# Seven-product units of 512 columns with the products added up in PSUM, and their sums of weight blocks made by accumulating DMA transfers

## The chip, the cores and the metric

The kernel runs on one core of one Trainium2 chip. The metric is the device time of one execution in microseconds (us). Three runs of the kernel before gave 1854.23, 1854.59 and 1855.96 us; the median is 1854.59 us. The engines are TensorE (PE), VectorE (DVE), ScalarE (ACT), GpSimd (POOL) and SyncE (SP, which here only issues transfers).

## The reference

A trunk of two layers over 512 tokens of width 1024. Every layer normalizes the rows and multiplies them by one wide input matrix. Its columns feed five branches A to E, and five gate paths of 512 columns and five merge paths of 1024 columns. Each branch output is multiplied by its gate, projected, weighted by its merge gate, and added up:

```
for l in range(DEPTH):                                     # 2 layers
    xn = rms_norm(h, norm_g[l])
    (..., gates, merge) = jnp.split(xn @ w_in[l], offsets, axis=-1)
    branches = (dsa_branch(...), mla_branch(...), diff_branch(...), sgu_branch(...), memory_branch(...))
    mixed = functools.reduce(jnp.add, [
        jax.nn.sigmoid(merge[:, :, n]) * ((o * jax.nn.silu(gates[:, :, n])) @ w_branch[l, n])
        for n, o in enumerate(branches)])
    h = h + mixed @ w_out[l]
return rms_norm(h, final_norm_g)
```

All is fp32. The change concerns the products `xn @ w_in[l]` for the gate and merge columns of branches A and C alone: 512 + 1024 columns for each of the two branches, in each of two layers.

## The kernel before

**Products.** Weights are loaded as raw fp32 tiles of 512 KB by SP, and each is split in two parts: `wh` is a rounded copy made on ACT, `wl` the rest, a subtraction on DVE or POOL. Activations are split likewise (`xh`, `xl`). Every product is three matmuls (`three`, L484 to L487): high by high, high by low, low by high. What is made from one raw tile is called a granule; a plain unit takes two or more of them.

**Order of the work.** The string `ORDER` lists the units of a layer; they are traced in that order, and each engine runs its instructions in one row. The attention work is a side stream that `Pace` mixes in between products by planned times. `begin` (L428) prepares a granule: it issues the loads of the next ones on SP and starts the split of the granule after it.

**The seven stage.** At a layer's end stand the units of branches A and C (tokens after `xs`). They use seven products of half blocks instead of eight. The rows are 512 tokens by 1024; their four half blocks (token halves by row halves) are combined beforehand into `t1`, `t2`, `t3` and `t4` (`x_prep`, `x_swap`). The weights' four blocks a11, a12, a21, a22 are combined into s1 = a21 + a22, s2 = s1 - a11, a11 - a21 and a12 - s2. `unit_s` (L509 to L530) does 256 columns by 512 tokens: `seven_steps` (L363 to L390) makes the four sums on POOL (L380) and splits the seven blocks: copies on ACT (L371), subtractions on DVE or, for the second block, on POOL (L373). Each of the seven products has its own PSUM tile, of 12 matmuls of 128x256. ACT copies the first out (L526), and DVE adds the others into `st` (L528). Gates then go through a tanh (L1373) and a product on DVE (L1374), and a product with the branch output on POOL (L1375). Merge gates go through a tanh (L1414), and are multiplied with the projected branch (L1403) and added to `acc` on POOL (L1411). Each merge unit of 256 columns is followed by one granule of the branch projection (`pm<-yh,wh`), of 24 matmuls of 128x512.

Of the kernel before, what the change touches and what calls it, by code (L numbers as in the profile page):

```python
# [39 lines left out]
GSET = (1,)  # L40
WSB = True
STB = True
# [15 lines left out]
class Pace:  # L58
    """Interleaves side streams (attention) with the dense products as they are traced."""
# [68 lines left out]
class Granule:  # L128
    """Up to four 128-row blocks of 256 columns of a weight, split in two fp32r parts."""

    def __init__(self, parts, n, width=256, raws=1):
        self.parts, self.n, self.width, self.raws = parts, n, width, raws


def trunk(tc, d, out, taps=None):
# [43 lines left out]
    def f32(ap):  # L179
        return ap.bitcast(F32)  # L180
# [13 lines left out]
    # ---- input rows, small vectors, constants  # L194
# [59 lines left out]
    # ---- rotary tables  # L254
# [42 lines left out]
    def rope(eng, x, j, ct, st, outs=None):  # L297
        """x [128, 2, h, 2H], token tiles 2j and 2j+1; rotated in place or into outs."""
# [19 lines left out]
    # ---- differential lambdas  # L318
# [20 lines left out]
    # ---- long lived tiles  # L339
# [7 lines left out]
    # ---- weights  # L347
    order, state = [], {"dma": 0, "split": 0, "slot": 0}

    def issue(upto):  # L350
        while state["dma"] < min(upto, len(order)):
            g = order[state["dma"]]
            g.raw = [wp.tile([128, 4, 256], F32, tag="raw", bufs=NRAW, name="raw") for _ in range(g.raws)]
# [9 lines left out]
    def seven_steps(g):  # L363
        """Seven combinations of the four 512 x 128 blocks of a granule, split, in the order of their products."""
        r0, r1 = g.raw
        a11, a21, a12, a22 = (r[:, :, c * 128:(c + 1) * 128] for r in (r0, r1) for c in range(2))
        g.prod = []

        def put(src):
            h, lo = (z.rearrange("p (k c) -> p k c", k=4) for z in wtile())  # L370
            A.activation(h, src, AF.Copy)  # L371
            yield
            (G if len(g.prod) in GSET else V).tensor_tensor(out=lo, in0=src, in1=f32(h), op=ALU.subtract)  # L373
            g.prod.append((h, lo))
            yield

        def comb(x, y, op):
            o = (blk(F32, "ws") if WSB else pp.tile([128, 512], F32, tag="p", name="ws")).rearrange(
                "p (k c) -> p k c", k=4)
            G.tensor_tensor(out=o, in0=x, in1=y, op=op)  # L380
            return o
        yield from put(a11)
        s1 = comb(a21, a22, ALU.add)
        s2 = comb(s1, a11, ALU.subtract)
        yield from put(s2)
        yield from put(comb(a11, a21, ALU.subtract))
        yield from put(s1)
        yield from put(comb(a12, s2, ALU.subtract))
        yield from put(a22)
        yield from put(a12)  # L390

    def split_steps(g):
        if g.raws == 2:
            yield from seven_steps(g)
            return
        g.raw = g.raw[0]
        g.h, g.l = [], []
        for a in range(0, g.n, 2):
            b = min(a + 2, g.n)
            h, lo = (z.rearrange("p (k c) -> p k c", k=2) for z in wtile())  # L400
            raw, hv, lv = g.raw[:, a:b, :g.width], h[:, :b - a, :g.width], lo[:, :b - a, :g.width]
            A.activation(hv, raw, AF.Copy)  # L402
            g.h.append(h)
            yield
            (G if a else V).tensor_tensor(out=lv, in0=raw, in1=f32(hv), op=ALU.subtract)  # L405
            g.l.append(lo)
            yield
# [40 lines left out]
    def gseven(w, c0):  # L448
        def parts(*raws):
            return [(r, w[k0 * 128:(k0 + 4) * 128, c0:c0 + 256].rearrange("(k p) c -> p k c", p=128))  # L450
                    for r, k0 in zip(raws, (0, 4))]
        g = Granule(parts, 4, 256, 2)
        order.append(g)
        return g
# [29 lines left out]
    def three(o, ah, al, bh, bl, st, sp):  # L484
        T.matmul(o, ah, bh, start=st, stop=False)  # L485
        T.matmul(o, ah, bl, start=False, stop=False)  # L486
        T.matmul(o, al, bh, start=False, stop=sp)  # L487

    def unit_t(gs, kts, rh, rl, evac, n=512, ms=2):
        """[cols, tokens]: column tiles of 128."""  # L490
# [9 lines left out]
    def unit_n(gs, kts, lh, ll, evac, nt=4):  # L500
        """[tokens, cols]: token tiles in pairs, 256 columns."""
# [7 lines left out]
    def unit_s(g, xb, evac):  # L509
        """Transposed 256 columns by 512 tokens in seven products of half blocks instead of eight."""  # L510
        def run():
            begin(g)
            th = [blk(F32, "st0"), blk(F32, "st1")] if STB else [tr(name="st0"), tr(name="st1")]
            c11, c12, c21, c22 = (t_[:, a:a + 256] for t_ in th for a in (0, 256))
            uses = {"11": [(c11, None)], "t2": [(c22, c11)], "t3": [(c21, c22)], "t1": [(c12, c22), (c22, c21)],
                    "22": [(c12, c12)], "t4": [(c21, c21)], "21": [(c11, c11)]}
            for n, b in enumerate(uses):
                o = psm("s7")[:, :256]
                while len(g.prod) <= n:
                    split_some()  # L520
                for kt in range(4):
                    three(o, g.prod[n][0][:, kt], g.prod[n][1][:, kt], *xb(b, kt), kt == 0, kt == 3)
                    tick(3 * 256 * 0.43)
                for dst, other in uses[b]:
                    if other is None:
                        A.activation(dst, o, AF.Copy)  # L526
                    else:
                        V.tensor_tensor(out=dst, in0=o, in1=other, op=ALU.add)  # L528
            evac(th)
        plan.append(run)  # L530
# [13 lines left out]
    # ---- norm of rows into transposed parts  # L544
# [3 lines left out]
    def norm_rows(rows, ss, gname, l, hi, lo, step=600.0):  # L548
        """rows: [128, 1024] tiles with their sums of squares; writes hi/lo[k] [128, 128 * len(rows)]."""
# [27 lines left out]
    # ---- attention  # L577
# [27 lines left out]
    def pv_causal(o, terms):  # L605
        """terms(kb) -> list of (stationary, part of P)."""
# [8 lines left out]
    def attend(steps, scores, norm, trans, pv, pv_rows=None):  # L615
        """steps: list of (unit, i, last); software pipelined over the steps."""
# [46 lines left out]
    # ================= layers  # L663
# [20 lines left out]
    def layer(l, mm):  # L684
# [5 lines left out]
        # -- memory keys and values  # L690
# [18 lines left out]
        # -- e_q, transposed, one head per column tile  # L709
# [73 lines left out]
        # -- columns 512:1636 in natural layout  # L783
# [114 lines left out]
        # -- latent attention operands  # L898
# [116 lines left out]
        # -- sparse attention  # L1015
# [109 lines left out]
        # -- differential attention, two of its four heads at a time  # L1125
# [93 lines left out]
        # -- spatial gating  # L1219
# [106 lines left out]
        # -- combinations of the half blocks of the normed rows  # L1326
        def x_prep():
            S["t2"] = [c4(F32R, "t2").rearrange("p (k c) -> p k c", k=4) for _ in range(2)]
            for n in ("t3", "t4"):
                S[n] = [[blk(name=n).rearrange("p (k c) -> p k c", k=2) for _ in range(2)] for _ in range(2)]  # L1330
            S["t1"] = [blk(F32, "t1f").rearrange("p (k c) -> p k c", k=2) for _ in range(2)]
            for k in range(4):
                f1, f2 = tr(name="xf1"), tr(name="xf2")
                G.tensor_tensor(out=f1, in0=f32(xh[k]), in1=f32(xl[k]), op=ALU.add)
                V.tensor_tensor(out=f2, in0=f32(xh[k + 4]), in1=f32(xl[k + 4]), op=ALU.add)
                t1 = S["t1"][k // 2][:, k % 2]
                V.tensor_tensor(out=t1, in0=f1[:, 256:], in1=f1[:, :256], op=ALU.subtract)
                V.tensor_tensor(out=f1[:, 256:], in0=f2[:, 256:], in1=f1[:, 256:], op=ALU.subtract)
                V.tensor_tensor(out=f1[:, :256], in0=f2[:, 256:], in1=t1, op=ALU.subtract)
                V.tensor_tensor(out=f2[:, :256], in0=f2[:, :256], in1=f1[:, :256], op=ALU.subtract)  # L1340
                split(S["t2"][0][:, k], S["t2"][1][:, k], f1[:, :256])
                split(S["t3"][0][k // 2][:, k % 2], S["t3"][1][k // 2][:, k % 2], f1[:, 256:])
                split(S["t4"][0][k // 2][:, k % 2], S["t4"][1][k // 2][:, k % 2], f2[:, :256])
# [6 lines left out]
        def xb(b, kt):  # L1350
            if b == "t2":
                return S["t2"][0][:, kt], S["t2"][1][:, kt]
            if b in ("t3", "t4"):
# [5 lines left out]
        # -- gate, project, merge  # L1359
# [3 lines left out]
        def gates(nm, us, seven=False):  # L1363
            bi = "ABCDE".index(nm)

            def ev(ps, u):
                if u == 0:
                    y["h"] = [c4(F32R, "yh").rearrange("p (k c) -> p k c", k=2) for _ in range(2)]
                    y["l"] = [c4(F32R, "yl").rearrange("p (k c) -> p k c", k=2) for _ in range(2)]
                for m in range(2):  # L1370
                    k = 2 * u + m
                    th, sg = tr(name="th"), tr(name="sg")
                    A.activation(th, ps[m], AF.Tanh, scale=0.5)  # L1373
# [234 lines left out]
```

## Time and profile before

| what | value |
|---|---|
| median of three runs | 1854.59 us |
| the profiled execution: its own time, its span | 1854.6 us, 1854.6 us |
| PE busy | 1784.2 us, 96% of the span |
| DVE, ACT, POOL busy | 1280.2, 1000.2, 730.9 us |
| mean granted clock of PE | 0.986 |
| seven stage of layer 0 | 693.5 to 888.0 us |
| seven stage of layer 1 | 1604.1 to 1802.5 us |

The span runs from the first instruction to the last, and nothing that the profile shows lies around it. A wait is put down to the work that ended last before the waiting instruction could go. PEclk of 1.00 is the full clock of PE (2.4 GHz), 0.50 the lower one (1.2 GHz). The names in a row are those of the program: `s<-xh,wh` is a product of the seven stage, `pm` a product of any other unit, `ws` a sum of weight blocks.

### The profile page before, as it was taken

The numbers are of one execution on the slowest core, as the hardware profiler recorded it, in microseconds if no ns is written. First come the engines' busy times: TensorE is split into PE (matmuls) and PEld (weight loads), VectorE is DVE, ScalarE is ACT, GpSimd is POOL, SyncE is SP. The second block draws the span as 40 slices with busy tenths as digits, with TensorE's granted clock in tenths as the row PEclk, the third lists the DMA queues.
The fourth block names the chain that finished last, engine by engine and source line by source line (L and its number), as shares of the span: only waits on it lengthen the run. The fifth ranks groups of instructions, "written<-read, shape, count | busy, mean of one in ns | idle before, by whom it ended". The sixth has DMA issues, their size and how long they took to land. (4 is left out here: it accounts for less than half of the span.)

```text
span 1854.6 us, 31211 instructions
## 1 busy us (share of the span) xinstructions
PE 1784.2 (96%) x11481; PEld 1613.9 (87%) x11481; DVE 1280.2 (69%) x2979; ACT 1000.2 (54%) x2247; POOL 730.9 (39%) x603
## 2 busy tenths in 40 slices
PE   7999999999999997999999999999999999899898
PEld 6998889889988777989999988898999887789888
DVE  7438656996755679899354477489775655998963
ACT  7447766437745434455355567653476454444443
POOL 4123111442312366885241321125341133778733
PEclk9999999999999998999999999999999999999999
DMA  6322222332222222334452332223322222233241
GB/s 211 92 69 78 86 69 69 97 97 70 58 58 69 80 58 69 99 95 136 131 177 58 75 89 79 57 80 103 103 58 58 58 80 58 59 91 109 85 148 69
DMA packets 167745, 161.43 MB, mean 87 GB/s; under 512 B 26036, under 2 KB 163304, under 8 KB 167592
## 3 DMA queue, kind: packets, MB, share of 16 engines
q1 hardware_dynamic: 164648, 149.21, 28.0%
q0 software_dynamic: 2944, 10.23, 1.6%
q8 instruction: 91, 1.49, 0.3%
q14 instruction: 62, 0.51, 0.1%
HBM read 155.22 MB, written 4.19 MB: 86 GB/s over the span
## 5 line engine op out<-in xcount | busy, mean ns | idle before, releaser
L405 POOL TENSOR_TENSOR wl<-raw,wh 128x512 fp32r<-128x512 f32 (+1 forms) x226 | 300.8, 1332 | 803.8 <-ACT wh L402 632.8
L402 ACT ACTIVATE wh<-raw 128x512 fp32r<-128x512 f32 (+1 forms) x460 | 285.3, 623 | 328.1 <-PE pm L486 161.6
L485 PE MATMUL pm<-wh,xh 128*128 128x256 f32 x1024 | 294.6, 288 | 0.9 <-ACT nat L1091 0.8
L486 PE MATMUL pm<-wl,xh 128*128 128x256 f32 x1024 | 293.3, 286 | 0.0
L487 PE MATMUL pm<-wh,xl 128*128 128x256 f32 x1024 | 293.2, 286 | 0.0
L405 DVE TENSOR_TENSOR wl<-raw,wh 128x512 fp32r<-128x512 f32 (+1 forms) x234 | 182.7, 782 | 144.5 <-ACT wh L402 140.1
L485 PE MATMUL pm<-xh,wh 128*128 128x512 f32 x656 | 259.2, 396 | 0.8 <-ACT mth L1392 0.5
L487 PE MATMUL pm<-xh,wl 128*128 128x512 f32 x656 | 256.9, 394 | 0.0
L486 PE MATMUL pm<-xl,wh 128*128 128x512 f32 x656 | 256.7, 391 | 0.0
L485 PEld LDWEIGHTS pm<-wh,xh 128*128 128x128 f32 x1024 | 195.1, 190 | 5.8 <-ACT nat L1091 1.6
L487 PEld LDWEIGHTS pm<-wh,xl 128*128 128x128 f32 x1024 | 195.2, 191 | 2.8 <-issue 1.7
L486 PEld LDWEIGHTS pm<-wl,xh 128*128 128x128 f32 x1024 | 195.3, 191 | 2.7 <-issue 1.2
L586 ACT ACTIVATE p<-p,nm 128x512 f32<-128x512 f32 (+1 forms) x192 | 107.2, 558 | 78.2 <-DVE nm L584 77.3
L485 PEld LDWEIGHTS pm<-xh,wh 128*128 128x128 f32 x656 | 123.7, 189 | 26.8 <-ACT mth L1392 1.1
L487 PEld LDWEIGHTS pm<-xh,wl 128*128 128x128 f32 x656 | 123.6, 188 | 26.5
L486 PEld LDWEIGHTS pm<-xl,wh 128*128 128x128 f32 x656 | 123.7, 189 | 23.8
L485 PE MATMUL s<-xh,wh 128*128 128x256 f32 x384 | 113.1, 295 | 25.2 <-ACT mth L1392 12.2
L485 PE MATMUL pm<-yh,wh 128*128 128x512 f32 x320 | 125.9, 394 | 5.3 <-DVE st L528 5.3
L486 PE MATMUL pm<-yl,wh 128*128 128x512 f32 x320 | 126.0, 394 | 0.0
L487 PE MATMUL pm<-yh,wl 128*128 128x512 f32 x320 | 122.6, 392 | 0.0
L486 PE MATMUL s<-xl,wh 128*128 128x256 f32 x384 | 111.4, 290 | 0.0
L487 PE MATMUL s<-xh,wl 128*128 128x256 f32 x384 | 110.6, 291 | 0.0
(378 smaller groups left out, 4756.5 us busy)
## 6 DMA issues: line engine op xcount, KB each, us to landing
raw<-w_in SPq DMA_DIRECT2D x192, 512.0 KB, 3.7
raw<-w_branch SPq DMA_DIRECT2D x40, 512.0 KB, 3.5
raw<-mem_w_kv SPq DMA_DIRECT2D x16, 512.0 KB, 5.6
raw<-w_out SPq DMA_DIRECT2D x16, 512.0 KB, 3.7
raw<-mla_w_uq SPq DMA_DIRECT2D x18, 128.0 KB, 2.7
xrow<-x SPq DMA_DIRECT2D x4, 512.0 KB, 7.9
raw<-mla_w_ukv SPq DMA_DIRECT2D x16, 128.0 KB, 2.7
h<-x POOLq DMA_DIRECT2D x4, 512.0 KB, 4.6
```

What stands on the lines that cost most here:

```text
L402: A.activation(hv, raw, AF.Copy)
L405: (G if a else V).tensor_tensor(out=lv, in0=raw, in1=f32(hv), op=ALU.subtract)
L485: T.matmul(o, ah, bh, start=st, stop=False)
L486: T.matmul(o, ah, bl, start=False, stop=False)
L487: T.matmul(o, al, bh, start=False, stop=sp)
L586: A.activation(p[:, :L], p[:, :L], AF.Exp, bias=nm, scale=scale, accum_out=s)
```

## The change

Seven-product units now take 512 columns by 512 tokens (`unit_o`), so a gate path is one unit (`oA`, `oC`) and a merge path two (`pA0`, `pA1`, `pC0`, `pC1`), 12 units in all. A block is 512 rows by 256 columns, one raw tile, and each product is 24 matmuls of 128x256. Products are added up in three PSUM tiles X, Y and Z, with signs moved into the blocks, so that a unit is evacuated by three ACT copies and three DVE operations of 128x512. The sums of weight blocks are made without an engine's arithmetic: SP loads a base block, and POOL issues transfers that add other blocks to it (`accum_op=ALU.add`, L362). A unit has six base loads and five such adds, 60 adds in all, of 512 KB each: two into s2, one into s1, one into t3, and a third into s2's buffer after s2 was split, which makes s4. All second parts of the seven stage are split on DVE. Raw tiles come from the pool `c4`, which grows from 6 to 12 tiles. The rest of a layer keeps its order.

```diff
-         "gD0 gD1 +df1 mD0 mD1 -df1 mD2 xp mD3 !xp xs gA0 gA1 mA0 mA1 mA3 mA2 gC0 gC1 mem mC0 mC1 mC3 mC2")
+         "gD0 gD1 +df1 mD0 mD1 -df1 mD2 xp mD3 !xp xs oA pA0 pA1 oC mem pC0 pC1")
-NB = 36
-NC4 = 6
+NB = 34
+NC4 = 12
-NRAW = 4
+COMB = "dma"
+    def issue_adds(k):
+        for g in order[k:min(k + 5, state["dma"])]:
+            n = len(g.adds)
+            while g.added < n and order.index(g) <= k + 1 + n - g.added:
+                dst, src = g.adds[g.added]
+                nc.gpsimd.dma_start(dst(), src, accum_op=ALU.add)
+                g.added += 1
     def begin(g):
         k = order.index(g)
         split_upto(k + 1)
         split_all()
         issue(k + 4)
+        issue_adds(k)
         split_upto(k + 2)
+    def goct(w, c0):
...
+            gs = [one("a11", a11), one("a12", a12), one("s2", None, a22, [a21, a11]), one("s1", None, a22, [a21]),
+                  one("t3", None, a21, [a11]), made(s4, adds=[((lambda: U["s2"]), a12)]), one("a22", a22)]
+    def unit_o(gs, xb, evac):
+        def run():
+            th = [c4(F32, "st").rearrange("p (m t) -> p m t", m=2) for _ in range(2)]
+            c11, c12, c21, c22 = (t_[:, :, a:a + 256] for t_ in th for a in (0, 256))
...
+            steps = [("X", "11", copy(c11)), ("Y", "21", plus(c11)), ("X", "t2", copy(c12)), ("Z", "t1", copy(c22)),
+                     ("X", "t3", neither(c22)), ("Z", "22", plus(c12)), ("X", "t4", None)]
+            for g, (bk, b, post) in zip(gs, steps):
+                begin(g)
...
+                for kt in range(4):
+                    for m in range(2):
+                        c = slice(m * 128, m * 128 + 128)
+                        three(o[:, m * 256:(m + 1) * 256], g.h[kt // 2][:, kt % 2, c], g.l[kt // 2][:, kt % 2, c],
+                              *xb(b, kt), new and kt == 0 and m == 0, kt == 3 and m == 1, True)
+                        tick(3 * 256 * 0.47)
         def x_prep():
...
-                G.tensor_tensor(out=f1, in0=f32(xh[k]), in1=f32(xl[k]), op=ALU.add)
+                V.tensor_tensor(out=f1, in0=f32(xh[k]), in1=f32(xl[k]), op=ALU.add)
...
+            G.tensor_tensor(out=sg, in0=sg, in1=oT[nm][k], op=ALU.mult)
```

**POOL at the end of branch A's gate, before.** `sg` is a gate, `ws` a sum of weight blocks in SBUF, `wl` a second part; the last two `sg` are those of the second gate unit.

```order
L380 TENSOR_TENSOR ws_8694<-raw_8402,ws_8656 128x512
L373 TENSOR_TENSOR wl_8659<-ws_8656,wh_8658 128x512
L1375 TENSOR_TENSOR sg_8776<-sg_8776,oA_5784 128x512
L1375 TENSOR_TENSOR sg_8783<-sg_8783,oA_6196 128x512
L380 TENSOR_TENSOR ws_8921<-raw_8634,raw_8635 128x512
L380 TENSOR_TENSOR ws_8923<-ws_8921,raw_8634 128x512
L380 TENSOR_TENSOR ws_8935<-raw_8634 128x512
L405 TENSOR_TENSOR wl_8808<-raw_8477,wh_8807 128x512
```

**The same place after.** The DMA rows are the adds: `raw_8485` is t3 of `oA`; `raw_8681` is s2 of `pA0` (three adds, the last two in one row), `raw_8733` its s1, `raw_8770` its t3; `raw_9027` is s2 of `pA1`.

```order
L362 DMA raw_8485<-w_in 128x4x256
L1446 TENSOR_TENSOR sg_8668<-sg_8668,oA_4980 128x512
L1446 TENSOR_TENSOR sg_8675<-sg_8675,oA_5353 128x512
L1446 TENSOR_TENSOR sg_8718<-sg_8718,oA_5784 128x512
L1446 TENSOR_TENSOR sg_8725<-sg_8725,oA_6196 128x512
L362 DMA raw_8681<-w_in 128x4x256
L362 DMA raw_8733<-w_in 128x4x256
L362 DMA raw_8770<-w_in 128x4x256
L362 DMA raw_8681<-w_in 128x4x256 x2
L383 TENSOR_TENSOR wl_8966<-raw_8878,wh_8965 128x512
L362 DMA raw_9027<-w_in 128x4x256
```

All four gates of `oA`, the last two of which wait for the unit's last product, now stand ahead of every add of `pA0`. Before, the sums of the next unit (`ws_8921` and on) stood behind the second gate unit's two multiplies as well, as instructions of POOL itself; the first unit's two multiplies stood further up.

**PE in `pA0`, after.** The unit's products in their order on PE: 21 (Y), t1 with s1 (Z, `wh_8811`), t2 with s2 (X, `wh_8777`), two matmuls of 22 with s4 (Z, `wh_8883`), t3 with the third sum (X, `wh_8848`), the rest of 22 and t4 (X).

```order
L548 MATMUL s7_8773<-xl7_130,wh_8750 128x256
...
L547 MATMUL s7_8844<-xh1_116,wh_8811 128x256
...
L547 MATMUL s7_8736<-t2_8263,wh_8777 128x256
...
L547 MATMUL s7_8844<-xh4_119,wh_8883 128x256
...
L547 MATMUL s7_8736<-t3_8267,wh_8848 128x256
...
L547 MATMUL s7_8736<-t4_8271,wh_8919 128x256
```

The first two matmuls of 22 stand ahead of t3, so that the whole of t3 comes after s4's add on PE, though it does not use s4.

## Rows read from the trace of the kernel before

**Rows 1.** The page, busy time of the engines.
```profile
PE 1784.2 (96%) x11481; PEld 1613.9 (87%) x11481; DVE 1280.2 (69%) x2979; ACT 1000.2 (54%) x2247; POOL 730.9 (39%) x603
```

**Rows 2.** Waits of PE: us in total, times, longest us.
```profile
PE s L485 <- DVE st L528: 17.1, 10, 3.5
PE s L485 <- ACT mth L1392: 12.2, 2, 6.1
...
PE pm L485 <- DVE st L528: 5.3, 3, 3.2
PE s L485 <- DVE mth L1403: 4.9, 2, 2.4
```

**Rows 3.** Windows: length, PE, PEld, DVE, ACT, POOL busy, PEclk, DMA share, GB/s.
```profile
693.50:888.00 194.50, 176.77 (x1223) 166.86 (x1223) 171.50 (x244) 96.14 (x179) 137.61 (x95) 0.95 0.34 103
1604.10:1802.50 198.40, 175.07 (x1209) 165.08 (x1209) 170.13 (x229) 90.71 (x163) 136.57 (x90) 0.95 0.32 95
...
696.10:702.90 6.80, 3.30 (x14) 3.06 (x14) 5.80 (x14) 5.33 (x13) 1.75 (x2) 0.50 0.28 77
...
1771.30:1778.00 6.70, 5.47 (x25) 5.47 (x26) 3.88 (x8) 1.33 (x3) 1.57 (x2) 0.50 0.48 159
```

**Rows 4.** Timeline of PE, start of layer 0's stage: start, duration, idle before.
```profile
699.60 0.58 PE L485 MATMUL s<-xh,wh 128*128 128x256 f32 x1 [6.09 <-ACT mth L1392]
...
700.20 0.41 PE L487 MATMUL s<-xh,wl 128*128 128x256 f32 x1
700.41 0.41 PE L485 MATMUL s<-xh,wh 128*128 128x256 f32 x1
...
705.40 0.36 PE L485 MATMUL s<-t,wh 128*128 128x256 f32 x1 [2.44 <-DVE mth L1403]
...
705.71 0.28 PE L487 MATMUL s<-t,wl 128*128 128x256 f32 x1
705.83 0.28 PE L485 MATMUL s<-t,wh 128*128 128x256 f32 x1
```

**Rows 5.** Lines by form, whole span: busy us, mean ns, idle before.
```profile
L405 DVE TENSOR_TENSOR wl<-raw,wh 128x512 fp32r<-128x512 f32 x230 | 181.0, 788 | 124.1 <-ACT wh L402 119.7 <-PE pS L487 1.7 <-PE pm L487 1.6
...
L373 DVE TENSOR_TENSOR wl<-raw,wh 128x512 fp32r<-128x512 f32 x72 | 93.6, 1302 | 0.6 <-ACT wh L371 0.5
...
L380 POOL TENSOR_TENSOR ws<-raw 128x512 f32<-128x512 f32 x48 | 79.1, 1648 | 15.6 <-DMA raw<-w_in 15.6
...
L528 DVE TENSOR_TENSOR st<-s,st 128x256 f32<-128x256 f32 x168 | 67.2, 415 | 12.1 <-PE s L487 10.8
...
L371 ACT ACTIVATE wh<-raw 128x512 fp32r<-128x512 f32 x72 | 44.9, 627 | 48.3 <-PE s L486 38.4 <-DVE acc L1406 7.3 <-issue 2.1
...
L373 POOL TENSOR_TENSOR wl<-ws,wh 128x512 fp32r<-128x512 f32 x24 | 37.7, 1570 | 17.9 <-ACT wh L371 17.9
...
L1411 POOL TENSOR_TENSOR acc<-acc,st 128x512 f32<-128x512 f32 x16 | 24.0, 1522 | 17.6 <-DVE st L1403 17.6
```

**Rows 6.** Timeline of ACT, the last tanh of branch A's gate in layer 0.
```profile
731.83 0.61 ACT L1373 ACTIVATE th<-st 128x512 f32<-128x512 f32 x1
```

**Rows 7.** Timeline of POOL, the two multiplies that end that gate.
```profile
732.73 3.37 POOL L1375 TENSOR_TENSOR sg<-sg,oA 128x512 f32<-128x512 f32 x2 [5.48 <-DVE sg L1374]
```

**Rows 8.** DMA: the weights' queue; issues with size and median us to landing.
```profile
q1 hardware_dynamic: 164648, 149.21, 28.0%
...
raw<-w_in SPq DMA_DIRECT2D x192, 512.0 KB, 3.7
...
h<-x POOLq DMA_DIRECT2D x4, 512.0 KB, 4.6
hscr<-h POOLq DMA_DIRECT2D x4, 512.0 KB, 2.9
...
wsr<-sgu_w POOLq DMA_DIRECT2D x4, 256.0 KB, 6.3
```

More of the change, by code (lines that the diff above doesn't have):

```diff
@@ L128, with __init__ @@
 class Granule:
-    def __init__(self, parts, n, width=256, raws=1):
+    def __init__(self, parts, n, width=256, raws=1, adds=(), sums=None):
         self.parts, self.n, self.width, self.raws = parts, n, width, raws
+        self.adds, self.added, self.sums = adds, 0, sums
 def trunk(tc, d, out, taps=None):
@@ L352, in issue @@
             g = order[state["dma"]]
-            g.raw = [wp.tile([128, 4, 256], F32, tag="raw", bufs=NRAW, name="raw") for _ in range(g.raws)]
+            g.raw = [c4(name="raw").rearrange("p (k c) -> p k c", k=4) for _ in range(g.raws)]
             for dst, src in g.parts(*g.raw):
@@ L361, in wtile @@
         return [wp.tile([128, 512], F32R, tag=f"{n}{i}", bufs=1, name=n) for n in ("wh", "wl")]
[L363 to L390, printed above, removed]
     def split_steps(g):
[L393 to L396, printed above, removed]
         g.h, g.l = [], []
@@ L399, in split_steps @@
             b = min(a + 2, g.n)
+            if g.sums is None:
+                raw = g.raw[0][:, a:b, :g.width]
+            else:
+                raw = yield from g.sums(a // 2)
             h, lo = (z.rearrange("p (k c) -> p k c", k=2) for z in wtile())
-            raw, hv, lv = g.raw[:, a:b, :g.width], h[:, :b - a, :g.width], lo[:, :b - a, :g.width]
+            hv, lv = h[:, :b - a, :g.width], lo[:, :b - a, :g.width]
             A.activation(hv, raw, AF.Copy)
@@ L404, in split_steps @@
             yield
-            (G if a else V).tensor_tensor(out=lv, in0=raw, in1=f32(hv), op=ALU.subtract)
+            (G if a and g.sums is None else V).tensor_tensor(out=lv, in0=raw, in1=f32(hv), op=ALU.subtract)
             g.l.append(lo)
@@ L446, in gcols, with block, one, parts @@
         return g
[L448 to L454, printed above, removed]
+    def goct(w, c0):
+        def block(i, j):
+            return w[i * 512:i * 512 + 512, c0 + 256 * j:c0 + 256 * j + 256].rearrange("(k p) c -> p k c", p=128)
+        a11, a21, a12, a22 = (block(i, j) for i in range(2) for j in range(2))
+        U = {}
+        def one(name, src, base=None, adds=()):
+            def parts(raw):
+                U[name] = raw
+                return [(raw, base if base is not None else src)]
+            def sums(p):
+                yield from ()
+                return U[name][:, 2 * p:2 * p + 2]
+            return Granule(parts, 4, raws=1, adds=[((lambda: U[name]), a) for a in adds], sums=sums)
+        def made(fn, parts=lambda *_: [], raws=0, adds=()):
+            return Granule(parts, 4, raws=raws, adds=adds, sums=fn)
+        def pc(name, p):
+            return U[name][:, 2 * p:2 * p + 2]
+        def add(o, x, y):
+            V.tensor_tensor(out=o, in0=x, in1=y, op=ALU.add)
+            return o
+        def fresh(name, p):
+            U[name, p] = blk(F32, name).rearrange("p (k c) -> p k c", k=2)
+            return U[name, p]
+        if COMB == "dve":
+            def load2(r0, r1):
+                U["a21"], U["a22"] = r0, r1
+                return [(r0, a21), (r1, a22)]
+            def s2(p):
+                add(fresh("s1", p), pc("a21", p), pc("a22", p))
+                yield
+                o = add(fresh("s2", p), U["s1", p], pc("a11", p))
+                yield
+                return o
+            def s1(p):
+                yield from ()
+                return U["s1", p]
+            def t3(p):
+                o = add(pc("a21", p), pc("a21", p), pc("a11", p))
+                yield
+                return o
+            def s4(p):
+                o = add(U["s2", p], U["s2", p], pc("a12", p))
+                yield
+                return o
+            def last(p):
+                yield from ()
+                return pc("a22", p)
+            gs = [one("a11", a11), one("a12", a12), made(s2, load2, 2), made(s1), made(t3), made(s4), made(last)]
+        elif COMB == "part":
+            def s2(p):
+                o = add(fresh("s2", p), pc("s1", p), pc("a11", p))
+                yield
+                return o
+            def load_s1(raw):
+                U["s1"] = raw
+                return [(raw, a22)]
+            def s1(p):
+                yield from ()
+                return pc("s1", p)
+            def s4(p):
+                o = add(U["s2", p], U["s2", p], pc("a12", p))
+                yield
+                return o
+            gs = [one("a11", a11), one("a12", a12),
+                  made(s2, load_s1, 1, [((lambda: U["s1"]), a21)]), made(s1),
+                  one("t3", None, a21, [a11]), made(s4), one("a22", a22)]
+        else:
+            def s4(p):
+                yield from ()
+                return pc("s2", p)
+            gs = [one("a11", a11), one("a12", a12), one("s2", None, a22, [a21, a11]), one("s1", None, a22, [a21]),
+                  one("t3", None, a21, [a11]), made(s4, adds=[((lambda: U["s2"]), a12)]), one("a22", a22)]
+        order.extend(gs)
+        return gs
@@ L507, in unit_n, with copy, plus, neither @@
         unit(gs, kts, body, nt // 2, evac)
-    def unit_s(g, xb, evac):
+    def unit_o(gs, xb, evac):
         def run():
[L512 to L520, printed above, removed]
-                for kt in range(4):
[L522 to L529, printed above, removed]
+            th = [c4(F32, "st").rearrange("p (m t) -> p m t", m=2) for _ in range(2)]
+            c11, c12, c21, c22 = (t_[:, :, a:a + 256] for t_ in th for a in (0, 256))
+            bank = {}
+            def copy(dst):
+                return lambda o: A.activation(dst, o, AF.Copy)
+            def plus(dst):
+                return lambda o: V.tensor_tensor(out=dst, in0=o, in1=dst, op=ALU.add)
+            def neither(dst):
+                return lambda o: V.scalar_tensor_tensor(out=dst, in0=o, scalar=-1.0, in1=dst, op0=ALU.mult,
+                                                        op1=ALU.subtract)
+            steps = [("X", "11", copy(c11)), ("Y", "21", plus(c11)), ("X", "t2", copy(c12)), ("Z", "t1", copy(c22)),
+                     ("X", "t3", neither(c22)), ("Z", "22", plus(c12)), ("X", "t4", None)]
+            for g, (bk, b, post) in zip(gs, steps):
+                begin(g)
+                new = bk not in bank
+                if new:
+                    bank[bk] = psm("s7")
+                o = bank[bk]
+                for kt in range(4):
+                    for m in range(2):
[3 more added lines that the diff above has]
+                        tick(3 * 256 * 0.47)
+                o = o.rearrange("p (m t) -> p m t", m=2)
+                if post is not None:
+                    post(o)
+                evac(b, th, o)
@@ L1384, in merges, with gated @@
-        def merges(nm, us, last=False, seven=False):
-            bi = "ABCDE".index(nm)
+        def gated(nm, k, src):
+            if k == 0:
+                y["h"] = [c4(F32R, "yh").rearrange("p (k c) -> p k c", k=2) for _ in range(2)]
+                y["l"] = [c4(F32R, "yl").rearrange("p (k c) -> p k c", k=2) for _ in range(2)]
+            th, sg = tr(name="th"), tr(name="sg")
+            A.activation(th, src, AF.Tanh, scale=0.5)
+            V.scalar_tensor_tensor(out=sg, in0=th, scalar=1.0, in1=src, op0=ALU.add, op1=ALU.mult)
+            G.tensor_tensor(out=sg, in0=sg, in1=oT[nm][k], op=ALU.mult)
+            split(y["h"][k // 2][:, k % 2], y["l"][k // 2][:, k % 2], sg)
@@ new lines, in merged @@
+        def merged(k, th, ps, last):
+            first = acc[k] is None
+            if first:
+                acc[k] = blk(F32, "acc")
+            dst = acc[k] if first else th
+            V.scalar_tensor_tensor(out=dst, in0=th, scalar=1.0, in1=ps, op0=ALU.add, op1=ALU.mult)
+            if first:
+                return
+            if last:
+                V.tensor_tensor(out=acc[k], in0=acc[k], in1=dst, op=ALU.add)
+                M.setdefault("h", {})[k] = blk(name="mxh")
+                M.setdefault("l", {})[k] = blk(name="mxl")
+                split(M["h"][k], M["l"][k], acc[k])
+            else:
+                G.tensor_tensor(out=acc[k], in0=acc[k], in1=dst, op=ALU.add)
@@ L1392, in ev_m @@
                         A.activation(th[m], ps[m], AF.Tanh, scale=0.5)
-                def ev_b(ps, th=th, u=u):
-                    for m in range(2):
-                        k = 2 * u + m
-                        first = acc[k] is None
-                        if first:
-                            acc[k] = blk(F32, "acc")
-                            dst = acc[k]
-                        else:
-                            dst = th[m]
-                        V.scalar_tensor_tensor(out=dst, in0=th[m], scalar=1.0, in1=ps[m], op0=ALU.add, op1=ALU.mult)
-                        if not first:
-                            if last:
-                                V.tensor_tensor(out=acc[k], in0=acc[k], in1=dst, op=ALU.add)
-                                M.setdefault("h", {})[k] = blk(name="mxh")
-                                M.setdefault("l", {})[k] = blk(name="mxl")
-                                split(M["h"][k], M["l"][k], acc[k])
-                            else:
-                                G.tensor_tensor(out=acc[k], in0=acc[k], in1=dst, op=ALU.add)
@@ L1440, in layer @@
         last_l = l == DEPTH - 1
-        seven = False
         for tok in ORDER.split():
```

119 lines of the change are left out of this document (64 added, 55 removed).

## The prediction

> **What bounds the kernel now.** I read the page's busy times first: PE is busy 96% of the span, and no other engine over 69% [rows 1]. So the kernel can only gain where PE idles or runs at its lower clock, and any new wait of PE adds its full length. Next the windows by stage. In the two seven stages PE is busy 176.77 of 194.50 us and 175.07 of 198.40 us [rows 3]: 17.7 + 23.3 = 41.0 us idle. The waits of PE name what ended those idle times: the additions of products in `st` on DVE (17.1 and 5.3 us), the start of the stage behind ACT's `mth` (12.2 us in two waits) and a DVE merge right after it (4.9 us in two) [rows 2]; these four make 39.5 of the 41.0. The timeline shows the start in layer 0: a gap of 6.09 us, then one of 2.44 [rows 4].
>
> Gaps have a second price. After the 6.09 us one, matmuls follow one another every 0.21 us (700.20 to 700.41); before long it is 0.12 (705.71 to 705.83) [rows 4], and the stretch from 696.1 to 702.9 has the granted clock 0.50, PE's lower level of 1.2 GHz, with 3.30 us of PE work in it; the last of seven such stretches, at 1771.3, holds 5.47 us [rows 3]. The seven hold 31.0 us of work, half of it lost: 15.5 us. They follow ten gaps of 2.4 us or more (the first two are those of [rows 4]), so such a gap costs about 1.55 us beyond itself.
>
> If every wait of the two stages went and the clock stayed up, the span would be 1854.6 - 41.0 - 15.5 = 1798.1 us. The profiled execution equals the median of the runs (1854.59), so no correction stands between the two.
>
> **What the change takes away.** PE's work is not changed: 7 products of 24 matmuls per 512 columns replace 14 of 12. On DVE the 168 additions of 415 ns go (67.2 us) [rows 5]; per unit three operations of twice the size come, 36 in all, at about 0.7 us some 25 us. POOL loses its 96 sums (48 of them are in the row of 1648 ns) and 24 second parts of 1570 ns [rows 5], 158 + 38 = 196 us of its stages; the latter go to DVE. DVE's second parts of raw blocks took 1302 ns here against 788 ns elsewhere in the kernel for the same shape [rows 5], while POOL worked at the same time; with POOL nearly idle I take 0.8 us, so that the 24 new ones are paid for by the old ones. So DVE, at 171.50 of 194.50 us the second busiest engine of the stage [rows 3], falls by 21 us at least (half of 67 less 25). The starting waits on `mth` and DVE go too, since `x_prep` runs on an undisturbed DVE and the PSUM tiles number three a unit. I count all 41.0 + 15.5 us as gone and then charge what is new.
>
> **What it adds.** Sixty transfers that add 512 KB each. Call L the time from issue to landing of one. The order on the engines sets what waits for them. The unit's clock is this: a product of 24 matmuls lasts 24 x 0.12 = 2.9 us, a unit 20.2.
>
> *`pA0` and `pC0`.* Their five adds stand on POOL behind the four gate multiplies of `oA` or `oC`, and POOL takes its instructions in turn. In the kernel before, 4.3 us pass from the start of the last tanh (731.83) to the end of the last multiply (732.73 + 3.37) [rows 6, 7]; a copy and another tanh of 0.6 each [rows 6] come ahead, 5.5 us; behind the splits queued on ACT and DVE for `pA0` I take 7.0 us after `oA`'s last product. PE meanwhile does 11 and 21 and is ready for t1 at 5.8. The add for s1 goes out second, at 7.9, and with its split (0.63 on ACT, about 0.8 on DVE [rows 5]) t1 starts at about 9.6 + L. s2 needs two adds one after the other, for both write one buffer: landed at 7.5 + 2L. The third, into the same buffer, must also wait for s2's four split operations, 1.9 us: out at 9.4 + 2L, landed at 9.4 + 3L, split at 11.3 + 3L. Two matmuls of 22 that use s4 stand on PE ahead of t3, so t3, 22 and t4 (8.7 us) all start after that: the unit ends at 20.0 + 3L instead of 20.2. Stall: 3L - 0.3, at four places.
>
> *`oA`.* Its s4 add stands behind the `acc` additions of the last unit before the stage, two of 1.5 us [rows 5] that wait for that unit's last product. Normally s4's add has two products, 5.8 us, less a split of 1.1: 4.7 us of cover. The 3.0 us on POOL leave 1.7. Stall: L - 1.7, at two places.
>
> *`pA1`, `oC`, `pC1`.* Their early adds go out during the unit before; only s4's is issued inside, with the 4.7 us of cover. Stall: L - 4.7 where that is above nothing, at six places.
>
> **How large L is.** The trace has no transfer that adds, and it must read its destination as well. Transfers that POOL issued took 2.9 us (`hscr<-h`) or 4.6 us (`h<-x`) for 512 KB in long rows, and 6.3 us for 256 KB in 512 runs of 512 bytes (`wsr`) [rows 8]; the adds are 512 KB in 512 runs of 1 KB. Plain loads by SP of just these blocks took 3.7 us [rows 8]. Below, 2.9 us; above, two plain transfers one behind the other, 9.2. I take 5.5, between 4.6 (same size and issuer) and 6.3 (same number of runs).
>
> The Trainium skill ("DMA: Bandwidth & Descriptors", section on the anatomy of one DMA) fits a transfer issued by GpSimd as 2.0 us plus its bytes over 436 KB per us; for 512 KB that would be an estimated 3.2 us, and the sum below would come to about 1848. No run here shows an add; the plain 4.6 us of `h<-x` [rows 8] is already slower than that rule, so I don't take it as the likeliest, and it is the first rival.
>
> **The sum.** With L = 5.5: `oA` 2 x 3.8 = 7.6; `pA0` and `pC0` 4 x 16.2 = 64.8; the others 6 x 0.8 = 4.8; together 77.2 us. Twelve gaps of 2.4 us or more (one per `oA`, two or three per `pA0` and `pC0`) at 1.55: 18.6. So 1798.1 + 77.2 + 18.6 = 1893.9, and I predict 1894 us. With 4.6 it is 59.8 us of stalls and about 15 for the clock: 1873. With 6.3, 93.2 and 19: 1910.
>
> The removed waits (56.5 us with the clock) are thus paid back and more, because a sum that POOL made in 1.65 us [rows 5] without leaving its row now takes a transfer's latency three times in series, right where the unit before has only just ended.
>
> Small things cost nothing unless their cover fails: POOL's issuing of 60 adds (well under 1 us each, in 196 us set free); 24 more base loads on SP, which has nothing else to do there; 12 tiles of `c4` for raw blocks, `st` and `y`, where a load may have to wait for a tile. If loads came late, each would add its 3.7 us [rows 8] at most to a unit's start.
>
> **Rivals.**
>
> *Quick adds.* If an add lands in about 2.9 us, `pA0` and `pC0` stall 8.4 us each, `oA` 1.2, the others nothing: 36.0 us, with four gaps over 2.4 us (6.2): 1840. Even then most stalls stand, so 1798 would need the gate multiplies off the path as well. This is the side on which the kernel becomes faster; it decides below L = 3.5 (22.2 us of stalls a layer and about 11 for the clock: 1854). For it speaks that one POOL transfer of the size took 2.9 us; against it that this one wrote to memory, in rows of 4 KB, while the two that read took 4.6 or longer [rows 8].
>
> *Adds bound by throughput.* The weights' queue used 28.0% of 16 engines over 1854.6 us for 149.21 MB [rows 8], so 512 KB take 1.8 us of all engines. A layer's stage has 44 loads (80 us) and 30 adds: 55 us at the same price, 109 at the double one of reading and writing the destination. Against about 200 us that fills most of the engines, where now the DMA share is 0.34 and 0.32 [rows 3]; adds then queue, and L = 9.2 gives 7.5 x 2 + 27.3 x 4 + 4.5 x 6 = 151 us, with 16 gaps (25): 1974. For it: loads and adds come in bunches at the start of units. Against it: at the average, even the doubled load fits.
>
> *The change is a wash.* If L is 3.5 to 3.7, or if the multiplies leave POOL sooner (5.5 instead of 7.0 us takes 6 us off) and L is about 4, stalls and gains cancel: 1850 to 1860. It needs two sizes to meet.
>
> *Another engine becomes the bound.* DVE takes 24 second parts from POOL (19 us at 0.8), and each wait on DVE behind its 171.50 us [rows 3] would remain. It stays below PE by some 25 us a stage (176.77 less about 150), so this could keep perhaps 17 us of the old `st` waits: 1911, inside the range.
>
> **How the numbers follow.** Main case (L of 4 to 7.5): 0.56, from 1860 to 1935. Quick adds: 0.18. Throughput: 0.14. Wash: 0.08, of which a quarter faster, half within, a quarter slower. DVE the bound: 0.04. A measurement of this kernel tells 0.2% (3.7 us) from no change. Faster: 0.18 + 0.02 = 0.20; same 0.04; slower 0.56 + 0.14 + 0.04 + 0.02 = 0.76. The range for 8 in 10 leaves out the faster half of the quick adds and the slower half of the throughput case: 1838 to 1965. Cases of both signs are in it; the likeliest one's own range is 1860 to 1935.
>
> **What would show it.** Right: in the changed profile PE's long waits in the stage end with splits of `raw` tiles at the t1, t2 and t3 of `pA0` and `pC0`, 12 to 20 us a unit in two or three gaps, eight or more stretches at clock 0.50, no wait on `st` adds; the adds' landing time about 5.5 us; second parts on DVE near 0.8 us. Wrong: a landing time under 3.5 us, or adds of `pA0` that are issued before the last multiply of `oA`; gaps in `pA1` or `pC1` as long as in `pA0` would speak for throughput.

## The result, and the profile after

The changed kernel takes 1948.76 us (median; 1946.62 to 1949.33) against 1855.28 us for the kernel before, measured beside it: 1.0506 times as long, 95% interval 1.0493 to 1.0518. The profiled execution took 1946.7 us. Slower was forecast, but at 1894 us, with 1965 at the top of the range: the loss is 92.1 us between the two profiles, where 39 were forecast.

The page after, busy times and DMA queues (packets, MB, share of 16 engines), and the issues with their median time to landing:

```profile
PE 1808.2 (93%) x11481; PEld 1634.3 (84%) x11481; DVE 1167.6 (60%) x2879; ACT 1011.7 (52%) x2253; POOL 598.1 (31%) x535
...
q1 hardware_dynamic: 177320, 161.79, 27.7%
q0 software_dynamic: 34624, 41.69, 12.3%
...
raw<-w_in SPq DMA_DIRECT2D x216, 512.0 KB, 3.7
raw<-w_in POOLq DMA_DIRECT2D x60, 512.0 KB, 7.8
```

Against [rows 1] DVE is relieved by 112.6 us, where two times 21 were worked out as the least, and POOL by 132.8, with the issues of the 60 adds counted in its busy time. What is new is the last row: an add lands after 7.8 us in the median, where 5.5 were taken. The windows of the two seven stages, each up to the same place in PE's work as in [rows 3] (length, PE, PEld, DVE, ACT, POOL busy, PEclk, DMA share, GB/s):

```profile
696.30:929.75 233.45, 184.30 (x1223) 172.45 (x1222) 118.38 (x175) 97.11 (x171) 78.11 (x61) 0.91 0.74 163
1655.50:1894.56 239.06, 187.00 (x1210) 175.50 (x1209) 115.02 (x159) 92.33 (x155) 76.84 (x60) 0.86 0.71 159
```

PE runs as many matmuls, and DVE falls by 53 and 55 us, but the stages are longer by 39.0 and 40.7 us, which is 79.7 of the 92.1. Their mean clock is lower, and DMA is at 0.74 and 0.71 instead of 0.34 and 0.32. The waits of PE (total, times, longest) against [rows 2]:

```profile
PE s L547 <- ACT wh L380: 99.3, 19, 11.2
...
PE pT L678 <- DVE p L1265: 7.0, 2, 3.8
```

The waits on `st` and `mth` are gone but for 0.2 and 0.9 us, as forecast. One wait stands for the rest of the story: PE waits for the split `wh` of a raw tile, which waits for an add to land. The chain in `pA0` of layer 0, on PE:

```profile
739.67 0.58 PE L547 MATMUL s<-xh,wh 128*128 128x256 f32 x1 [11.18 <-ACT wh L380]
...
753.91 0.44 PE L547 MATMUL s<-xh,wh 128*128 128x256 f32 x1 [5.07 <-ACT wh L380]
```

On POOL:

```profile
724.64 3.38 POOL L1446 TENSOR_TENSOR sg<-sg,oA 128x512 f32<-128x512 f32 x2 [1.23 <-DVE sg L1445]
728.65 1.64 POOL L1446 TENSOR_TENSOR sg<-sg,oA 128x512 f32<-128x512 f32 x1 [0.62 <-DVE sg L1445]
730.24 3.92 POOL L362 DMA_DIRECT2D raw<-w_in  x3
736.81 1.28 POOL L362 DMA_DIRECT2D raw<-w_in  x1 [2.66 <-DMA raw<-w_in]
746.78 1.28 POOL L362 DMA_DIRECT2D raw<-w_in  x1 [8.69 <-DVE wl L383]
```

And on ACT:

```profile
738.99 1.15 ACT L380 ACTIVATE wh<-raw 128x512 fp32r<-128x512 f32 x2 [8.03 <-DMA raw<-w_in]
...
744.53 1.67 ACT L380 ACTIVATE wh<-raw 128x512 fp32r<-128x512 f32 x3 [2.20 <-DMA raw<-w_in]
...
752.71 1.15 ACT L380 ACTIVATE wh<-raw 128x512 fp32r<-128x512 f32 x2 [4.76 <-DMA raw<-w_in]
```

The gate's last multiply ends at 730.3. Three adds go out behind it (s2's first, s1, the third sum). s1 is split at 738.99 and lets t1 go at 739.67, after 11.18 us; s2's second add goes out at 736.81, when the first has landed, and is split at 744.53; s4's goes out at 746.78 behind that split and is split at 752.71, and only then 22 and t3 go on, at 753.91. That is the chain of the prediction, step by step.

### The profile page after: what moved, and what is told of

Same layout as the page of the kernel before. It is cut to its first block, busy times and chain, and to the rows that moved or that the text cites. A ratio compares the mean times of both kernels' runs of the same rounds, so it can differ in the third digit from the quotient of the medians.

```text
span 1946.7 us, 31020 instructions
## 1 busy us (share of the span) xinstructions
PE 1808.2 (93%) x11481; PEld 1634.3 (84%) x11481; DVE 1167.6 (60%) x2879; ACT 1011.7 (52%) x2253; POOL 598.1 (31%) x535
## 3 DMA queue, kind: packets, MB, share of 16 engines
q0 software_dynamic: 34624, 41.69, 12.3%
## 5 line engine op out<-in xcount | busy, mean ns | idle before, releaser
L380 ACT ACTIVATE wh<-raw 128x512 fp32r<-128x512 f32 (+1 forms) x628 | 385.5, 623 | 545.6 <-PE pm L548 195.7
L383 DVE TENSOR_TENSOR wl<-raw,wh 128x512 fp32r<-128x512 f32 (+1 forms) x402 | 296.9, 751 | 344.7 <-ACT wh L380 341.9
L547 PEld LDWEIGHTS s<-xh,wh 128*128 128x128 f32 x384 | 77.7, 202 | 66.9 <-ACT wh L380 66.6
L547 PE MATMUL s<-t,wh 128*128 128x256 f32 x288 | 92.8, 322 | 34.4 <-ACT wh L380 34.3
```

What stands on the lines that cost most here:

```text
L383: (G if a and g.sums is None else V).tensor_tensor(out=lv, in0=raw, in1=f32(hv), op=ALU.subtract)
L547: T.matmul(o, ah, bh, start=st, stop=False, skip_group_check=shared)
```

## The experiments

**The sums on DVE instead of adds by DMA** (the kernel's own alternative; 24 base loads go with the adds, the rest of the change stays).

```diff
-COMB = "dma"
+COMB = "dve"
```

> The changed kernel with its own alternative for the sums: no accumulating transfers, all four sums by DVE additions of 128x512 (8 per unit, 96 in all, about 0.69 us each as the other DVE operations of this size in the changed trace: 66 us more DVE work). All else (units of 512 columns, PSUM accumulation, x_prep) as changed. Theory 'the 60 adds alone cost the time': the 99 us of PE waits in the stages and most of the lower clock go; about 1800 to 1825 us, so faster than the kernel before. Rival 'the 512-column units themselves cost time (three banks, longer evacuation, a later start)': 1850 or more, with PE waiting for DVE's st rows or for wl.

Measured: 1852.79 us, 0.9986 of the kernel before (0.9976 to 0.9995). The first theory is right on where the loss lies (some 96 us go with the adds) and missed its time by 28 us, since the waits did not all go. The time is one that the rival expected (1850 or more); of the rival's signs PE shows waits of 8.6 us on `wl`:

```profile
PE s L547 <- ACT wh L380: 23.0, 12, 4.9
PE s L549 <- DVE wl L383: 8.6, 10, 2.3
```

The longest on `wh`, 3.8 to 4.9 us, stand at `pA0` and `pC0` again. DVE there, and POOL:

```profile
720.38 1.77 DVE L186 TENSOR_TENSOR yl<-sg,yh 128x512 fp32r<-128x512 f32 x1
...
726.65 0.68 DVE L186 TENSOR_TENSOR yl<-sg,yh 128x512 fp32r<-128x512 f32 x1
727.25 0.68 DVE L451 TENSOR_TENSOR s<-raw 128x512 f32<-128x512 f32 x1
```

```profile
719.93 3.38 POOL L1446 TENSOR_TENSOR sg<-sg,oA 128x512 f32<-128x512 f32 x2 [1.23 <-DVE sg L1445]
```

The unit's first sum (L451) stands on DVE behind the whole gate. The gate's `yl` takes 1.77 us while POOL multiplies, and 0.68 after POOL has ended. The Trainium skill ("SBUF — State Buffer", section on who interferes with whom) says that a DVE instruction with two inputs in SBUF contends with a POOL instruction that reads SBUF; these two rows agree.

**Only one add for each of two sums.**

```diff
-COMB = "dma"
+COMB = "part"
```

> Two of the sums (s1, third) by one accumulating transfer each, s2 and s4 by DVE: 24 adds instead of 60, none of them in series. Theory 'latency in series behind the gate multiplies': each pA0 and pC0 still waits for one landing, issue at 7.3 us after the gate unit plus 7 us, less the 5.8 us of its first two products: about 10 us at four places, the six other units nothing; with the clock some 1850 us. Rival 'engine throughput of the adds': with 2 in place of 5 adds per unit they land in about 4 to 5 us, waits of 6 us at four places: about 1835.

Measured: 1867.12 us, 1.0062 (1.0040 to 1.0084). `pA0` and `pC0` wait 8.0 to 8.4 us, `oA`, `pA1` and `oC` 0.9 to 3.9:

```profile
PE s L547 <- ACT wh L380: 48.7, 20, 8.4
...
raw<-w_in POOLq DMA_DIRECT2D x24, 512.0 KB, 7.1
```

Taking away 36 of 60 adds shortens the landing by 0.7 us only, which is against the second theory's 4 to 5: at `pA0` and `pC0` the two that are left still go out within 2 us of each other, and elsewhere a single one among loads takes up to 9.7 us. The first was short by 17 us, of which the waits outside `pA0` and `pC0` are the larger part.

**Plain copies in place of adds** (the sums are left out).

```diff
-                nc.gpsimd.dma_start(dst(), src, accum_op=ALU.add)
+                nc.gpsimd.dma_start(dst(), src)
```

> The 60 transfers as plain copies: same places, sizes and waits, no addition (so the sums are left out, and each block is just overwritten). In the changed trace a transfer that adds has packets worth 3.5 us of all 16 engines (10.7 % of 1946.7 us for 60), a base load of the same size 1.75 us. Theory 'reading and writing the destination makes them slow': landing falls from 7.8 to about 4.6 us and the time to about 1885. Rival 'it is POOL's issue of 512 runs and the software queue, not the addition': landing stays at 7 us or more, the time at 1935 to 1950.

Measured: 1863.63 us, 1.0050 (1.0035 to 1.0065).

```profile
PE s L547 <- ACT wh L380: 43.5, 10, 9.4
...
q0 software_dynamic: 11584, 41.69, 6.8%
...
raw<-w_in POOLq DMA_DIRECT2D x60, 512.0 KB, 4.9
```

The same bytes in the same places, without the addition: landing 4.9 instead of 7.8 us, near the first theory's 4.6, and 86 us of 92 gone, 21 more than its time of 1885 allows. The queue's share goes with it. POOL's other transfers take 1.6% of 1854.6 us in the kernel before, 29.7 us; what is left for the 60 is (12.3% of 1946.7 - 29.7) / 60 = 3.5 us of all 16 engines' packet time for an add, and (6.8% of 1860.7 - 29.7) / 60 = 1.6 us for a copy. By the packets of that queue (2944 in the kernel before) an add has 528 and a copy 144; whether the time goes with the number of packets or with reading the destination is not separated here.

**The gate multiplies on DVE**, so that no add stands behind them.

```diff
-            G.tensor_tensor(out=sg, in0=sg, in1=oT[nm][k], op=ALU.mult)
+            (V if nm in "AC" else G).tensor_tensor(out=sg, in0=sg, in1=oT[nm][k], op=ALU.mult)
```

> The four gate multiplies of oA and of oC on DVE instead of POOL, so that the adds of pA0 and pC0 no longer stand behind them; all five adds per unit stay. Theory 'place on POOL plus latency in series': the first wait of pA0 and pC0 (11.2 us) falls to 4 to 6 us, about 25 us and a little clock in all: about 1915 to 1922. Rival 'throughput of the DMA engines bounds these units': the adds start earlier but land as much later, under 8 us gained: 1938 or more.

Measured: 1917.94 us, 1.0330 (1.0313 to 1.0348): some 31 us less than the changed kernel, as the first theory had it. PE in `pA0`, layer 0:

```profile
733.48 0.39 PE L547 MATMUL s<-t,wh 128*128 128x256 f32 x1 [1.64 <-ACT wh L380]
...
744.24 0.58 PE L547 MATMUL s<-t,wh 128*128 128x256 f32 x1 [4.05 <-ACT st L581]
```

The waits of 11.18 and 5.07 us become 1.64 and 4.05 (the latter is put down to ACT's copy of `st`), so the first falls further than the theory had it; the median landing stays at 7.9 us. The waits in `pA0` and `pC0` fall from 66.1 to 26.5 us in all, while those of the other units grow from 33.3 to 44.5. One place keeps a wait of 8.5 us, `pC0` of layer 0. There the adds stand on POOL behind another operation, a small power (`rstd`) of the normalization of the memory rows, which only layer 0 has and which waits for DVE:

```profile
838.89 1.66 POOL L244 TENSOR_TENSOR rstd<-rstd,mhalf 128x1 f32<-128x1 f32 x2 [21.94 <-DVE rstd L248]
840.51 3.93 POOL L362 DMA_DIRECT2D raw<-w_in  x3
```

**The transfers alone.**

```
one:  load a block by SP; then nc.gpsimd.dma_start(t, block, accum_op=ALU.add)
half: the same with half of the block      wide: with 128 rows of 4 KB
tri:  three adds at once, into three tiles
mix:  an add with three loads by SP at once
```

> Transfers by themselves, with none of the reference computed; blocks of w_in of 512 KB in 512 runs of 1 KB, each alone on the queues: a load by SP (lsp), one by POOL (lpl), an add on a landed block (one), an add of half a block (half), an add in 128 rows of 4 KB (wide), two adds into one block (ser), three adds into three blocks at once (tria, trib, tric), an add with three loads at once (mix, load). Theory 'throughput': an add alone lands in about 2 + 3.5 = 5.5 us, half in under 4, the last of three at once after 10 us or more, mix at 8 or more. Rival 'latency': an add alone takes 7 us or more, half nearly as long, and three at once land within 1 to 2 us of one alone (plus POOL's issue of 1.3 us each).

```profile
load<-w_in SPq DMA_DIRECT2D x12, 512.0 KB, 4.7
ser<-w_in POOLq DMA_DIRECT2D x8, 512.0 KB, 5.8
lsp<-w_in SPq DMA_DIRECT2D x4, 512.0 KB, 3.6
lpl<-w_in POOLq DMA_DIRECT2D x4, 512.0 KB, 4.0
...
one<-w_in POOLq DMA_DIRECT2D x4, 512.0 KB, 5.8
...
wide<-w_out POOLq DMA_DIRECT2D x4, 512.0 KB, 5.1
...
trib<-w_in POOLq DMA_DIRECT2D x4, 512.0 KB, 5.8
tria<-w_in POOLq DMA_DIRECT2D x4, 512.0 KB, 7.7
tric<-w_in POOLq DMA_DIRECT2D x4, 512.0 KB, 9.7
...
mix<-w_in POOLq DMA_DIRECT2D x4, 512.0 KB, 9.6
...
half<-w_in POOLq DMA_DIRECT2D x4, 256.0 KB, 4.4
```

Alone an add lands in 5.8 us, near the 5.5 of the forecast. In company it takes longer: of three issued some 0.75 us apart, in the order b, a, c, each lands about 2.7 us after the one before, and one beside three loads takes 9.6. Throughput is right, with a fixed part: from 4.4 us for 256 KB (under 4 was expected) and 5.8 for 512 KB, an estimated 3.0 us and 2.8 for each 512 KB.

**Half of each add** (the other half of each sum is left out).

```diff
-                nc.gpsimd.dma_start(dst(), src, accum_op=ALU.add)
+                nc.gpsimd.dma_start(dst()[:, :2], src[:, :2], accum_op=ALU.add)
```

> The changed kernel with each add covering half of its block (rows of k 0 and 1 only; the rest of each sum is left out): same 60 transfers at the same places, half the bytes. Theory 'throughput of the DMA engines': landing falls from 7.8 to about 4.5 us and the time to 1865 to 1885. Rival 'a fixed latency of an add': landing stays at 6.5 us or more, the time at 1925 or more.

Measured: 1863.07 us, 1.0050 (1.0031 to 1.0068), just below the first theory's span; waits 43.9 us in 12, landing 4.9:

```profile
PE s L547 <- ACT wh L380: 43.9, 12, 9.3
...
raw<-w_in POOLq DMA_DIRECT2D x60, 256.0 KB, 4.9
```

So an add of half the bytes costs what a whole plain copy does, in landing and in time. A latency that is the same for any size is ruled out as the cause.

**Both undone: plain copies, and the gate multiplies on DVE.**

```diff
-                nc.gpsimd.dma_start(dst(), src, accum_op=ALU.add)
+                nc.gpsimd.dma_start(dst(), src)
-            G.tensor_tensor(out=sg, in0=sg, in1=oT[nm][k], op=ALU.mult)
+            (V if nm in "AC" else G).tensor_tensor(out=sg, in0=sg, in1=oT[nm][k], op=ALU.mult)
```

> Both earlier edits at once: the 60 transfers as plain copies (the additions are left out) and the gate multiplies of oA and oC on DVE. Theory 'two separate causes, place in POOL's row and the slow add': the first waits of pA0 and pC0, 8.2 to 9.4 us with plain copies alone, fall by the time the multiplies held POOL, to 1 to 3 us; 1860.7 less some 30 us: 1828 to 1838, close to the 1798 us without any wait plus about 20 of waits and 10 for the clock. Rival 'the place costs only because adds queue' : plain copies are quick enough anyway, under 10 us gained: 1850 or more.

Measured: 1833.35 us, 0.9876 (0.9855 to 0.9898). This lies in the first theory's span. The 30 us of the multiplies' place come off again, on top of the copies' gain, so the two causes are separate. The first waits of `pA0` and `pC0` are 1.64 us at three of the four places; the 6.7 us stand in `pC0` of layer 0, behind the same `rstd`.

```profile
PE s L547 <- ACT wh L380: 18.0, 8, 6.7
```

**Versions that could be used: the gate multiplies on DVE, with the sums on DVE or on POOL.**

```diff
-COMB = "dma"
+COMB = "dve"
-            G.tensor_tensor(out=sg, in0=sg, in1=oT[nm][k], op=ALU.mult)
+            (V if nm in "AC" else G).tensor_tensor(out=sg, in0=sg, in1=oT[nm][k], op=ALU.mult)
```

> No adds by DMA: the sums on DVE as in the run before with 1852.8 us, and the gate multiplies of oA and oC on DVE too, so that POOL no longer slows DVE there (yl 1.78 us beside POOL, 0.68 alone). Theory 'what is left of the loss is the gate chain ahead of pA0's and pC0's sums': the first wait of those units falls from 4.9 to 1 to 2 us, some 15 us and a little clock: 1832 to 1842. Rival 'the place is the same, only the engine differs': DVE still does the multiplies ahead of the sums, 1847 to 1853.

The second has one line more, in the function that adds two blocks:

```diff
-            V.tensor_tensor(out=o, in0=x, in1=y, op=ALU.add)
+            G.tensor_tensor(out=o, in0=x, in1=y, op=ALU.add)
```

> As the run beside it, with the sums on POOL, which then does nothing else in the gate units. Theory 'POOL can make the sums ahead of time, since its row is free': first waits of pA0 and pC0 near nothing, but DVE's second parts go back to about 1.2 us: 1825 to 1845. Rival 'the slowing of DVE by POOL costs more than the place': 1850 or more, with PE waiting for wl.

Measured: with the sums on DVE 1842.52 us, 0.9938 (0.9926 to 0.9950), with the sums on POOL 1849.93 us, 0.9976 (0.9967 to 0.9985). The first is faster than both kernels, by 0.6% and 5.5%.

```profile
PE s L549 <- DVE wl L383: 13.6, 10, 2.3
PE s L547 <- ACT wh L380: 12.2, 15, 1.8
```

These are its waits; the longest on `wh` is 1.8 us instead of 4.9. With the sums on POOL PE waits 18.7 us on `wh`, up to 4.0, and 10.9 on `wl`. The first came out half a microsecond beyond the slow end of what its theory expected (1832 to 1842). The second lies 5 us beyond its theory's span and at the edge of the rival's (1850 or more); its waits on `wl` are no longer than with the sums on DVE, so neither theory is shown.

## Why the prediction was wrong in size

**Right.** The mechanism, its places and the gains. The end of the gate multiplies came 7.3 us after `oA`'s last product (723.0; forecast 7.0). The total without stage waits, 1798 us, holds: the run with both causes undone, 1834.9 us in its profile, has some 21 us of waits on `wh` and `wl` in the stages and some 18 us of PE work there at the lower clock; 1798.1 + 21 + 9 is within 7 us of it. The table sets the waits of the timeline (layer 0, layer 1, in us) against the sum's terms:

| unit | forecast | measured |
|---|---|---|
| `oA` | 3.8 | 3.9, 5.3 |
| `pA0` | 16.2 | 16.7, 16.3 |
| `pA1` | 0.8 | 4.6, 4.6 |
| `oC` | 0.8 | 3.6, 3.4 |
| `pC0` | 16.2 | 16.7, 16.4 |
| `pC1` | 0.8 | 2.3, 5.6 |

**The step that failed** is "How large L is": one time of 5.5 us for every add. That is nearly the landing of an add that nothing delays: 5.8 alone, and 6.0 in the median of the 26 adds that go out in the kernel while no other add is under way. The other 34 go out behind an add that has not landed, and their median is 8.4 (6.7 to 10.4), so that all 60 make 7.8. The three adds of `pA0` that go out together at 730.24 land 2.7 and 2.6 us one after the other, as in the run of the transfers alone (the last line of the view of `raw` on POOL from 730.2 to 733):

```profile
DMA to landing us min/median/max: 6.0/7.9/9.8
```

Three copies at the same place land after 4.8 to 6.1 us. The forecast had adds that queue, and the doubled engine time, only in a rival of 0.14, "adds bound by throughput", at L = 9.2 and 1974 us; the truth lies between the two. Of the 52.8 us between 1893.9 and 1946.7 the stalls make 22.1, the clock 15.4 and a wait outside the stages 11.9:

- `pA1`, `oC` and `pC1`: 4.8 us forecast, 24 measured. The forecast had one add, s4's, go out inside these units, with 4.7 us of cover. Two go out, 0.8 us apart, and the second lands after 7.9 to 10.4 us: in `pA1` they are issued at 780.25 and 781.04, the second lands at 790.7, and PE's wait ends at 791.4. The wait is before a product of a `t` block, so by the order of the products it is for t3's sum rather than s4.
- The clock: 18.6 us forecast for twelve gaps at 1.55. There were 16 gaps of over 2 us, and by windows of 1 us 68 us of the stages' PE work ran at the lower clock, 31 before: 34 us lost, 2.1 a gap.
- A wait outside the stages that was not priced: `oA`'s early adds stand on POOL among the small operations (`dr`, L244) of branch C's attention. There s2's second add waits until the first, issued at 647.82, has landed, 6.0 us later; this holds up `dr`, that holds up DVE, and that PE:

```profile
647.82 1.35 POOL L362 DMA_DIRECT2D raw<-w_in  x1 [2.03 <-DMA raw<-w_in]
...
654.11 1.32 POOL L362 DMA_DIRECT2D raw<-w_in  x1 [3.32 <-DMA raw<-w_in]
654.94 1.08 POOL L244 TENSOR_TENSOR dr<-dr,mhalf 128x1 f32<-128x1 f32 x1
```

```profile
656.05 0.79 DVE L1282 TENSOR_SCALAR don<-don,dr 128x128 f32<-128x128 f32 x1 [3.42 <-POOL dr L244]
656.26 0.58 DVE L1265 SCALAR_TENSOR_TENSOR p<-p,r 128x128 f32<-128x128 f32 x1
```

```profile
657.01 0.30 PE L678 MATMUL pT<-ident,p 128*128 128x128 f32 x1 [3.22 <-DVE p L1265]
```

7.0 us in two waits, and about 4.9 us of clock around them (13.2 us of PE work at the lower clock there, 3.4 before). The wait is 2.3 us with half adds and under 1 with copies, and not among the waits of the runs without adds. That one wait was not undone by itself.

Together: waits 99.3 - 41.0, clock 34 - 15.5, outside 7.0 + 4.9 make 88.7 of the 92.1 us; 3.4 us stay open.

`pA0` and `pC0` came out at 16.3 to 16.7 although L was larger. In `pA0` of layer 0 the three adds of s2's buffer took 6.6, 7.7 and about 5.9 us by the rows above, 20.2 in all, for which the formula gives 19.9. Part of the difference is that the unit's products ran at half clock between the waits (4.2 us of work, 2.1 lost), so that PE arrived later; the rest is open. The forecast's figure is right by errors that cancel, not by its L: that is luck.

The rule of the Trainium skill that the prediction weighed ("DMA: Bandwidth & Descriptors", the anatomy of one DMA; an estimated 3.2 us for this size) was rightly not followed: a copy by POOL alone lands in 4.0 us and an add in 5.8. The quick rival needed L under 3.5. Issuing an add was taken at well under 1 us of POOL's time; its row takes 1.27.

## What to carry to other kernels

Price a transfer that stands in series by its landing time in company, above all beside others of its kind that go out with it, and its engine time by what it does to its destination; the time of a plain load is only a lower bound for both. Before a sum is moved from an engine to a transfer, read in the order what stands ahead of its issue on that engine and whether the transfers must follow one another: here that place cost 30 us, and the adds 86 more than copies. An engine that a change relieves is worth nothing by itself; with DVE freed by the larger units, DVE could make the sums and the gates, 0.6% faster than before.

## What the runs showed of the hardware

An add of 512 KB in 512 runs of 1 KB lands in 5.8 us alone, a copy by POOL in 4.0, a load by SP in 3.6; with rows of 4 KB the add takes 5.1. The row of an issue on POOL takes 1.27 us for an add and 0.75 us for a copy, though adds that follow one another went out 0.75 us apart:

```profile
21.00 0.77 POOL L72 DMA_DIRECT2D lpl<-w_in  x1 [3.74 <-DVE sink L53]
...
48.51 1.28 POOL L64 DMA_DIRECT2D one<-w_in  x1 [8.88 <-DVE sink L53]
```

Beside an add, three loads by SP landed in 4.7 us (3.6 alone) while the add took 9.6, so the add bore most of the delay.
